# A two-block transformer on one core: paired attention heads in turns, split weight products in another order, later gates, routing without GpSimd

## The chip, the cores and the metric

The kernel runs on one core of a Trainium2 chip. The time is that of the device for one execution, in microseconds (us), as the median of the runs shown below. A core has a matrix engine (TensorE, PE in the profile), a vector engine (VectorE, DVE), a scalar engine (ScalarE, ACT), a general one (GpSimd, POOL), and a queue that issues the transfers (SyncE, SP). Each engine takes its instructions in the order of its own list and waits on semaphores for the others.

## The reference

The input is 256 tokens of 1024 columns. Everything is fp32.

```python
for l in range(2):
    x = x + 0.5 * swiglu(rmsnorm(x, ffn1_norm[l]), wg, wu, wd)      # d_ff 2816
    h = rmsnorm(x, mix_norm[l]) @ w_in[l]
    o = concat([mla(h_a), nsa(h_b), diff(h_c)])                      # 6, 6 and 4 heads
    x = x + o @ w_out[l]
    x = x + 0.5 * swiglu(rmsnorm(x, ffn2_norm[l]), wg, wu, wd)
h = concat([meta_tokens, rmsnorm(x, final_norm)])                    # 16 + 256 tokens
p = rmsnorm(h, norm_mix_2) @ w_in_2                                  # z, x, B, C, dt, b, c, h
y = concat([group_norm(ssd(x, B, C, dt) * silu(z)), group_norm(b * conv(c * h))])
h = h + y @ w_out_2
u = rmsnorm(h, norm_ffn_2)                                           # 4 groups x 4 experts, top 2 of one group
h = h + sum_e combine[:, e] * ((silu(u @ w_gate[e]) * (u @ w_up[e])) @ w_down[e])
out = rmsnorm(h, norm_final_2)[16:]
```

## The kernel before

**Split products.** A product of fp32 operands is made of three: each weight tile arrives as `st`, ScalarE rounds it to a high half `wh` (line 166), VectorE, or GpSimd for the tiles that the table `LOW` names, subtracts to get the low half `wl` (line 167). The activations have halves as well (`xhl`, `ohl`, `uhl`, `hh` and `hl`). `mm3` multiplies wh by the high half, wh by the low half, and wl by the high half, 256 columns each. `mm2` has both halves of the activations side by side: wh by 512 columns, wl by 256; the result then lies in two parts of a bank, and VectorE adds both.

**Order.** The code is written as tasks, and a scheduler orders the instructions of each engine; `behind(i)` holds what stands in it until the instruction i has been placed. TensorE does nearly all work: FFN1, the mixer (projection `win`, heads, `w_out`) and FFN2 for both layers, then the second block and the experts.

**The heads.** The softmax of a head gives a transposed P in a tile `PT`. The products of PT and the values of two heads go into one bank `opair`, one head in its partitions 0 to 63, the other in 64 to 127 (`pv_pair`). In the heads of NSA the products of the compressed branch (`cpt`) go into the same two halves. The fp32 products there are made in several passes, so one line of code is several matmul rows of the profile.

**From w_out to FFN2.** `w_out` makes eight tiles `wo` of 128x256, which VectorE adds to the residual stream `xT` (lines 966 and 967). From xT come the operand pieces `xhl` (lines 267 and 268) and the squares for the norm. Where FFN2 begins, its first four weight tiles are multiplied k by k into four `gu` banks, and two of these banks lie in the PSUM space of wo.

**The second block** follows the table `PART2`: step "z" makes the z columns, "u" the normed operand (xT times two factors gives `u`, its halves are `uhl`), "r" rewrites xT by the final norm of the first block, "d" the dt columns, "b", "x" the convolved ones (`proj`, then `cv`), "w" the last product. The z gate is tanh on ScalarE (`zth`) and a scalar_tensor_tensor on VectorE (line 1106).

**Routing.** `moe_tokens` runs for each half of the tokens: two copies, the sum of squares and its inverse root (`mss`, `mr`), eight transposes (`h2T`, copied to `hT`), eight products for the `logits`. `moe` splits the tokens into hh (ScalarE) and hl (GpSimd, line 1615), finds ranks and `slots`, gathers (`xgp`), and starts the experts' sum `moe` with identity products of the tokens. Those of the second half of the tokens are held behind the last logits product.

```python
            for k in KO:
                self.mm2(p, wh[:, k], wl[:, k], ohl[:, k], k == KO[0], k == KO[7])
            xv = self.xT[:, 2 * b + j]
            nc.vector.tensor_add(xv, p[:, 0:T], xv)
            nc.vector.tensor_add(xv, p[:, T:2 * T], xv)
```

## Time and profile before

| | before |
|---|---|
| median of 3 runs | 1568.68 us |
| lowest and highest run | 1567.85 and 1570.5 us |
| the profiled execution | 1569.35 us |
| its span, first to last instruction | 1567.5 us |
| mean granted TensorE clock (1 is 2.4 GHz) | 0.986 |

The profiled execution is one run of the same program. Its span is what the trace shows; the rest of its time, 1.85 us, lies around it. A granted clock of 0.50 in a stretch means that TensorE ran at 1.2 GHz there.

### The profile page before, as it was taken

How to read it: one execution, taken by the hardware profiler on the slowest of the kernel's cores; microseconds unless marked ns; L12 is line 12 of the kernel's file. 1: busy time of each engine (PE TensorE's matmuls, PEld its weight loads, DVE VectorE, ACT ScalarE, POOL GpSimd, SP SyncE). 2: the span in 40 equal slices, each digit the busy share in tenths (PEclk: the TensorE clock that was granted, in tenths of full speed). 3: DMA queues.
4: the chain of work that ended last, by engine and by line, in shares of the span. 5: the costliest groups of instructions: out<-in, count | busy, mean ns of one | idle time of the engine just before them, and what ended most of it. 6: DMA issues, size and time to landing. Idle time of an engine off the chain costs nothing.

```text
span 1567.5 us, 25184 instructions
## 1 busy us (share of the span) xinstructions
PE 1514.2 (97%) x9842; PEld 1256.1 (80%) x9842; DVE 1035.7 (66%) x2024; ACT 731.1 (47%) x1385; POOL 96.5 (6%) x144
## 2 busy tenths in 40 slices
PE   8999999999999999999999899999799999999996
PEld 7999998768999989999886799999799987344432
DVE  7777776857677886777585777778988875122112
ACT  5555465745445555545664554557554442011011
POOL 0000000600000000000033000000410101000000
PEclk9999999999999999999999999999999998999998
DMA  7756664125555565656530455566443588999992
GB/s 249 247 183 193 176 169 143 47 66 175 188 189 183 167 191 187 193 191 175 161 108 1 148 183 189 181 195 207 149 135 108 175 297 334 338 394 392 392 396 87
DMA packets 223558, 308.92 MB, mean 197 GB/s; under 512 B 20908, under 2 KB 167608, under 8 KB 223432
## 3 DMA queue, kind: packets, MB, share of 16 engines
q1 hardware_dynamic: 223128, 306.71, 58.7%
q8 instruction: 79, 1.29, 0.4%
q10 hardware_dynamic: 304, 0.53, 0.1%
q14 instruction: 47, 0.39, 0.1%
HBM read 306.16 MB, written 1.05 MB: 196 GB/s over the span
## 4 chain that ended last, share of the span: by engine, by line
PE 91%; DVE 6%; ACT 1%; issue 1%; DMA 0%; POOL 0%; ACTq 0%; DVEq 0%
PE gu L98 32%; PE acc L98 16%; PE proj L98 7%; PE win L98 6%; PE gate L98 4%; PE y L98 4%; PE up L98 4%; PE h L98 3%; PE S L98 3%; PE opair L98 2%; PE wo L98 2%; PE zp L98 1%; DVE wl L167 1%; PE moe L98 1%; PE ptp L684 1%; PE xgp L98 1%
## 5 line engine op out<-in xcount | busy, mean ns | idle before, releaser
L167 DVE TENSOR_TENSOR wl<-st,wh 128x1024 fp32r<-128x1024 f32 (+1 forms) x370 | 447.5, 1219 | 209.4 <-ACT wh L166 198.6
L166 ACT ACTIVATE wh<-st 128x1024 fp32r<-128x1024 f32 (+1 forms) x382 | 399.2, 1059 | 346.2 <-PE gu L98 136.4
L98 PE MATMUL gu<-xhl,wh 128*128 128x512 f32 (+1 forms) x1440 | 496.3, 394 | 14.1 <-DVE xT L967 11.0
L98 PE MATMUL gu<-xhl,wl 128*128 128x256 f32 x1408 | 390.5, 281 | 0.0
L98 PEld LDWEIGHTS gu<-xhl,wh 128*128 128x128 f32 x1440 | 269.6, 191 | 74.2 <-issue 12.4
L98 PEld LDWEIGHTS gu<-xhl,wl 128*128 128x128 f32 x1408 | 266.0, 190 | 0.1
L98 PE MATMUL acc<-hx,wh 128*128 128x256 f32 x1408 | 252.1, 281 | 0.0
L98 PEld LDWEIGHTS acc<-hx,wh 128*128 128x128 f32 x1408 | 216.4, 189 | 1.6
L98 PE MATMUL acc<-hx,wl 128*128 128x256 f32 x704 | 197.0, 281 | 0.0
L98 PE MATMUL proj<-uhl,wh 128*128 128x272 f32 (+2 forms) x592 | 129.0, 309 | 7.2 <-DVE cv L1208 5.1
L98 PEld LDWEIGHTS acc<-hx,wl 128*128 128x128 f32 x704 | 132.7, 189 | 0.0
L98 PE MATMUL win<-wh,xhl 128*128 128x256 f32 (+1 forms) x576 | 109.5, 286 | 0.2 <-DVE xT L403 0.2
L98 PEld LDWEIGHTS proj<-uhl,wh 128*128 128x128 f32 x592 | 97.5, 195 | 12.3 <-ACT zth L1105 4.4
L98 PE MATMUL proj<-uhl,wl 128*128 128x272 f32 (+2 forms) x328 | 96.2, 294 | 0.0
L98 PEld LDWEIGHTS win<-wh,xhl 128*128 128x128 f32 x576 | 90.9, 191 | 3.8 <-issue 3.1
L98 PE MATMUL win<-wl,xhl 128*128 128x256 f32 (+1 forms) x288 | 82.2, 285 | 0.0
L387 ACT ACTIVATE hx<-up 128x512 fp32r<-128x512 f32 x44 | 27.8, 631 | 87.8 <-DVE up L386 87.8
L98 PEld LDWEIGHTS proj<-uhl,wl 128*128 128x128 f32 x328 | 63.5, 194 | 0.3
L726 POOL TENSOR_SCALAR P<-P,mx 128x128 f32<-128x128 f32 (+2 forms) x88 | 53.2, 620 | 65.4 <-DVE mx L719 46.2
L1790 DVE SCALAR_TENSOR_TENSOR ys<-y,rc,ys 128x512 fp32r<-128x512 f32 x16 | 11.8, 749 | 68.5 <-ACT ys L1607 68.0
L716 ACT ACTIVATE P<-S,mx 128x256 f32<-128x256 f32 (+2 forms) x128 | 48.8, 396 | 17.5 <-DVE mx L712 4.4
L98 PEld LDWEIGHTS win<-wl,xhl 128*128 128x128 f32 x288 | 55.0, 191 | 0.6 <-issue 0.3
(523 smaller groups left out, 2158.3 us busy)
## 6 DMA issues: line engine op xcount, KB each, us to landing
st<-ffn_wg SPq DMA_DIRECT2D x44, 1024.0 KB, 5.8
st<-ffn_wu SPq DMA_DIRECT2D x44, 1024.0 KB, 5.4
st<-ffn_wd SPq DMA_DIRECT2D x44, 1024.0 KB, 4.9
st<-w_in SPq DMA_DIRECT2D x36, 1024.0 KB, 5.4
st<-w_out SPq DMA_DIRECT2D x16, 1024.0 KB
mf<-expert_w_gate SPq DMA_DIRECT2D x25, 512.0 KB, 9.5
mf<-expert_w_down SPq DMA_DIRECT2D x21, 512.0 KB, 10.7
mf<-expert_w_up SPq DMA_DIRECT2D x18, 512.0 KB, 11.3
```

Of the source, the lines that this page charges most:

```text
L98: return self.nc.tensor.matmul(out, lhsT, rhs, start=start, stop=stop, skip_group_check=True)
L166: hi = self.nc.scalar.activation(hl[0], src, AF.Copy)
L167: sub = (self.nc.gpsimd if lo[i] == "p" else self.nc.vector).tensor_sub(hl[1], src, hl[0].bitcast(F32))
L387: nc.scalar.activation(hh, up, AF.Copy)
L684: tr(p[:, i * 128:(i + 1) * 128], b, ident)
L716: nc.scalar.activation(P[:, d], s[:, c], AF.Exp, bias=m[:, 0, i:i + 1], accum_out=m[:, 1, i:i + 1])
L726: (nc.gpsimd if key + str(i) in "c0 c1 c2 d0 d1 m0 w0 w1".split() else nc.vector).tensor_scalar(P[:, d], P[:, d], r[:, i:i + 1], None, op0 ...
L1790: V.scalar_tensor_tensor(yl, py[half], rc[:, 1:2], yh.bitcast(F32), op0=OP.mult, op1=OP.subtract)
```

## The change

1. The products of a pair of heads stand together in TensorE's list: the products of the half 64 to 127 lead, and all others of the pair stand behind the first of them (`in_turns`). The compressed products are treated in the same way.
2. At the head of FFN2 (and of the second FFN1) the sixteen wh products of k 0 to 3 come first, then their sixteen wl products, then k 4 to 7 bank by bank.
3. `w_out` uses `mm3`, so that VectorE has one addition for each tile instead of two.
4. The tanh and the multiplication of the z gates become a step "q" behind x0, "r" moves to the end of its part, and their `behind(done)` goes.
5. `moe_tokens` does both halves: all hT copies on ScalarE, squares of the first half on ScalarE, hl on VectorE, all logits in one go, and all identity products held behind the last logits product.

```diff
@@ -31,9 +31,9 @@
 
 
 
-PART2 = ("z10 u z2 z3 d p4 b0 d r b1 d b2 b3 x0 x1 x2 s0 s0 x3 s0 c0 "
+PART2 = ("z10 u z2 z3 d p4 b0 d b1 d b2 b3 x0 q x1 x2 s0 s0 x3 s0 c0 "
          "h0 s1 s1 g0 s1 s2 s2 n0 c1 h1 s2 s3 g1 n1 s3 c2 h2 g2 s3 "
-         "| c3 h3 p5 g3 n2 y a w6 t0 t1 p7 t2 w0 n3 t3 % w1 p4 w5 w2 w4 p5 w3 w7")
+         "r | c3 h3 p5 g3 n2 y a w6 t0 t1 p7 t2 w0 n3 t3 % w1 p4 w5 w2 w4 p5 w3 w7")
 
 LOW = {k: "pp" for k in ["b3", "x0", "x1", "x2", "x3"]}
 LOW.update({k: "vp" for k in ["h3", "g2"]})
@@ -347,9 +347,16 @@
 
                 ws = [w for u in units for w in self.split(u, "n")]
                 ps = [self.bank(tag, "gu") for tag in "BBCC"]
-                for k, i in ([(k, i) for k in range(4) for i in range(4)]
-                             + [(k, i) for i in range(4) for k in range(4, KD)]):
-                    self.mm2(ps[i], ws[i][0][:, k], ws[i][1][:, k], xhl[:, k], k == 0, k == KD - 1)
+                high = lambda k, i: self.mm(ps[i], ws[i][0][:, k], xhl[:, k], k == 0, False)
+                low = lambda k, i: self.mm(ps[i][:, 0:T], ws[i][1][:, k], xh[:, k], False, k == KD - 1)
+                for part in (high, low):
+                    for k in range(4):
+                        for i in range(4):
+                            part(k, i)
+                for i in range(4):
+                    for k in range(4, KD):
+                        high(k, i)
+                        low(k, i)
                 return ps
             for i, u in enumerate(units):
                 for f, (wh, wl) in enumerate(self.split(u, "n", "vv")):
@@ -520,7 +527,7 @@
             return ap.tile([128, 2, n], F32, name=name, tag=tag or name, bufs=bufs)
 
         hA, hQ, hV, hC, hW = tok("hA", 352), tok("hQ", 768), tok("hV", 402), tok("hC", 512), tok("hW", 256)
-        oh, ol, ohl = self.pair("ohl")
+        oh, ol, _ = self.pair("ohl")
         B0, C0 = 352, 1522
         q0, kc0, vc0, ks0, vs0, kw0, vw0 = [B0 + c for c in (0, 384, 512, 640, 768, 896, 1024)]
         groups = [
@@ -697,11 +704,17 @@
 
         def pv_pair(o, key, first, last):
 
-            two = list(zip((o[0:64], o[64:128]), waiting.pop(key)))
-            for o_, (pt, v) in two:
-                self.mm(o_[:, 0:256], v[0], pt[:, 0:256], first, False)
-            for o_, (pt, v) in two:
-                self.mm(o_[:, 128:256], v[1], pt[:, 256:384], False, last)
+
+            two = list(zip((o[64:128], o[0:64]), waiting.pop(key)[::-1]))
+            in_turns([lambda o_=o_, pt=pt, v=v: self.mm(o_[:, 0:256], v[0], pt[:, 0:256], first, False) for o_, (pt, v) in two]
+                     + [lambda o_=o_, pt=pt, v=v: self.mm(o_[:, 128:256], v[1], pt[:, 256:384], False, last) for o_, (pt, v) in two])
+
+        def in_turns(products):
+
+            lead = products[0]()
+            with self.behind(lead.ins):
+                for product in products[1:]:
+                    product()
 
         def softmax(s, P, segs, gate=None, low=None):
 
@@ -854,8 +867,9 @@
             if h % 2:
                 o = self.bank("O", "opair")
                 pv_pair(o, "s", True, False)
-                for i, (c, v) in enumerate(waiting.pop("c")):
-                    self.mm(o[i * 64:(i + 1) * 64, 0:256], v, c[0:15], False, False)
+                c0, c1 = waiting.pop("c")
+                in_turns([lambda o_=o_, c=c: self.mm(o_, c[1], c[0][0:15], False, False)
+                          for o_, c in ((o[64:128, 0:256], c1), (o[0:64, 0:256], c0))])
             s = self.bank("S", "S")
             scores(s, qt, kw[:, g], kw[:, g, 0:128])
             P = ap.tile([128, 384], F32, name="P", tag="P", bufs=6)
@@ -961,10 +975,9 @@
             for j, (wh, wl) in enumerate(self.split(wo[b], "n")):
                 p = self.bank("WS"[j], "wo")
                 for k in KO:
-                    self.mm2(p, wh[:, k], wl[:, k], ohl[:, k], k == KO[0], k == KO[7])
+                    self.mm3(p[:, 0:T], wh[:, k], wl[:, k], oh[:, k], ol[:, k], k == KO[0], k == KO[7])
                 xv = self.xT[:, 2 * b + j]
                 nc.vector.tensor_add(xv, p[:, 0:T], xv)
-                nc.vector.tensor_add(xv, p[:, T:2 * T], xv)
             after(b)
 
 
@@ -1099,8 +1112,12 @@
         def z_gates(ids, ps):
             for b, p in zip(ids, ps):
                 for t in range(2):
+                    ACT(z[:, t, b * 256:(b + 1) * 256], p[:, t * 256:(t + 1) * 256], scale=R[:, t:t + 1])
+
+        def z_silu():
+            for b in range(4):
+                for t in range(2):
                     zv = z[:, t, b * 256:(b + 1) * 256]
-                    ACT(zv, p[:, t * 256:(t + 1) * 256], scale=R[:, t:t + 1])
                     th = ap.tile([128, 256], F32, name="zth", tag="zth", bufs=2)
                     nc.scalar.activation(th, zv, AF.Tanh, scale=0.5)
                     nc.vector.scalar_tensor_tensor(zv, th, 1.0, zv, op0=OP.add, op1=OP.mult)
@@ -1115,8 +1132,7 @@
                 u = ap.tile([128, T], F32, name="u", tag="q", bufs=4)
                 nc.vector.scalar_tensor_tensor(u, self.xT[:, k], self.gfm[:, k:k + 1], rb[:, 1], op0=OP.mult, op1=OP.mult)
                 ACT(uh[:, k, NM:], u)
-                low_u = nc.vector.tensor_sub(ul[:, k, NM:], u, uh[:, k, NM:].bitcast(F32))
-            return low_u.ins
+                nc.vector.tensor_sub(ul[:, k, NM:], u, uh[:, k, NM:].bitcast(F32))
 
         def residual_norm():
             for k in range(KD):
@@ -1409,16 +1425,15 @@
                 if k == "z":
                     zs = z_blocks([int(c) for c in name[1:]])
                     if len(zs[0]) == 1:
-                        with self.behind(done):
-                            z_gates(*zs)
+                        z_gates(*zs)
                 elif k == "u":
                     norms()
-                    done = u_operand()
-                    with self.behind(done):
-                        z_gates(*zs)
+                    u_operand()
+                    z_gates(*zs)
+                elif k == "q":
+                    z_silu()
                 elif k == "r":
-                    with self.behind(done):
-                        residual_norm()
+                    residual_norm()
                 elif k == "d":
                     next(parts)
                 elif k == "b":
@@ -1453,8 +1468,7 @@
             self.operands.close()
             self.xp = self.pool(self.ctx, "operands2", side="right")
             self.moe_start(acc)
-            for t in range(2):
-                self.moe_tokens(t)
+            self.moe_tokens()
             yield
 
         return run()
@@ -1579,24 +1593,37 @@
         self.r = self.ap.tile([128, 2], F32, name="mr", tag="mr")
         self.logits = self.bank("C", "logits")
 
-    def moe_tokens(self, t):
+    def moe_tokens(self):
 
         nc, V, h2, hT, acc = self.nc, self.nc.vector, self.h2, self.hT, self.acc
-        V.tensor_copy(h2[:, t, 0:512], acc[t][0])
-        V.tensor_copy(h2[:, t, 512:1024], acc[t][1])
-        self.moe_sumsq(t, 0, self.th_)
-        self.moe_sumsq(t, 1, self.ht_)
-        self.moe_inv(t)
-        for k in range(0, KD, 4):
-            p = self.bank("B", "h2T")
-            for i in range(4):
-                nc.tensor.transpose(p[:, i * 128:(i + 1) * 128], h2[:, t, (k + i) * 128:(k + i + 1) * 128], self.identr[:].bitcast(F32))
-            (V.tensor_copy if t and not k else nc.scalar.copy)(hT[:, k:k + 4, t * 128:(t + 1) * 128],
-                                                               p[:].rearrange("p (k t) -> p k t", k=4))
-        for k in range(KD):
-            last = self.mm(self.logits[:, t * 20:(t + 1) * 20], hT[:, k, t * 128:(t + 1) * 128], self.gw[:, k],
-                           t == 0 and k == 0, k == KD - 1)
+        half = lambda i: slice(i * 512, (i + 1) * 512)
+        for t in range(2):
+            for i in range(2):
+                V.tensor_copy(h2[:, t, half(i)], acc[t][i])
+            if t == 0:
+                for i, j in enumerate((self.th_, self.ht_)):
+                    nc.scalar.activation(j, h2[:, t, half(i)], AF.Square, accum_out=self.ss[:, 2 * i + t:2 * i + t + 1])
+            for k in range(0, KD, 4):
+                p = self.bank("B", "h2T")
+                for i in range(4):
+                    nc.tensor.transpose(p[:, i * 128:(i + 1) * 128], h2[:, t, (k + i) * 128:(k + i + 1) * 128], self.identr[:].bitcast(F32))
+                nc.scalar.copy(hT[:, k:k + 4, t * 128:(t + 1) * 128], p[:].rearrange("p (k t) -> p k t", k=4))
+            if t:
+                for i, j in enumerate((self.th_, self.ht_)):
+                    V.scalar_tensor_tensor(j, h2[:, t, half(i)], 1.0, h2[:, t, half(i)], op0=OP.mult, op1=OP.mult,
+                                           accum_out=self.ss[:, 2 * i + t:2 * i + t + 1])
+            self.moe_inv(t)
+        for t in range(2):
+            for k in range(KD):
+                last = self.mm(self.logits[:, t * 20:(t + 1) * 20], hT[:, k, t * 128:(t + 1) * 128], self.gw[:, k],
+                               t == 0 and k == 0, k == KD - 1)
         self.routed = last.ins
+        for t in range(2):
+            nc.scalar.activation(self.hh[:, t], h2[:, t], AF.Copy)
+        self.low_half(0)
+
+    def low_half(self, t):
+        self.nc.vector.tensor_sub(self.hl[:, t], self.h2[:, t], self.hh[:, t].bitcast(F32))
 
     def moe(self):
 
@@ -1609,10 +1636,6 @@
                                                         self.slots_, self.th_, self.ht_)
         sm = ap.tile([128, 346], F32, name="route", tag="route")
         p = self.logits
-
-        for t in range(2):
-            ACT(hh[:, t], h2[:, t])
-            nc.gpsimd.tensor_sub(hl[:, t], h2[:, t], hh[:, t].bitcast(F32))
         units = self.load_pair(0)
 
 
@@ -1648,6 +1671,7 @@
         Ab = ap.tile([128, 2, 16], BF, name="Ab", tag="Ab")
         V.scalar_tensor_tensor(Ab[:].rearrange("p t (g e) -> p t g e", g=4), pe, 2.0,
                                og[:, :, :, None].to_broadcast([128, 2, 4, 4]), op0=OP.is_lt, op1=OP.mult)
+        self.low_half(1)
         p = self.bank("C", "rank")
         self.mm(p[:, 0:16], self.below, Ab[:, 0], True, False)
         self.mm(p[:, 16:32], self.onesb, Ab[:, 0], False, False)
@@ -1717,7 +1741,7 @@
 
         acc = self.acc = [[self.bank("A", f"moe{t}{i}") for i in range(2)] for t in range(2)]
         for t in range(2):
-            with self.behind(*((self.routed,) if t else ())):
+            with self.behind(self.routed):
                 for half in range(2):
                     self.mm(acc[t][half], ident, h2[:, t, half * 512:(half + 1) * 512], True, False)
 
```

The first place is TensorE's list in the NSA heads of layer 0; opair rows are the products of a pair, ptp the transposes of P, S the scores. Before, with the lead product of this pair 25 rows further up:

```order
L98 MATMUL S<-maskb,identb 128x128
L98 MATMUL opair<-PT,hV 64x256
L98 MATMUL opair<-PT,hV 64x128 x2
L98 MATMUL opair<-cpt,vcmp 64x256
L684 MATMUL ptp<-ident,P 128x128 x3
L98 MATMUL opair<-cpt,vcmp 64x256
L98 MATMUL opair<-PT,hV 64x256
```

After:

```order
L98 MATMUL S<-maskb,identb 128x128
L98 MATMUL opair<-PT,hV 64x256 x2
L98 MATMUL opair<-PT,hV 64x128 x2
L691 MATMUL ptp<-ident,P 128x128 x3
L98 MATMUL opair<-cpt,vcmp 64x256 x2
L691 MATMUL ptp<-ident,P 128x128 x3
```

The lead product now stands with the other of its size (`x2`), the two 128-column products follow, and the two cpt products stand together. Of the nine PT pairs of a layer eight were separated before and none is now; all three cpt pairs were separated.

The second place is VectorE's list at the end of layer 0's w_out: xT rows are the additions, xhl the low halves of the operand of FFN2. Before:

```order
L966 TENSOR_TENSOR xT<-wo,xT 128x256
L167 TENSOR_TENSOR wl<-st,wh 128x1024
L966 TENSOR_TENSOR xT<-wo,xT 128x256
L967 TENSOR_TENSOR xT<-wo,xT 128x256
L167 TENSOR_TENSOR wl<-st,wh 128x1024
L967 TENSOR_TENSOR xT<-wo,xT 128x256
L167 TENSOR_TENSOR wl<-st,wh 128x1024
L967 TENSOR_TENSOR xT<-wo,xT 128x256
L167 TENSOR_TENSOR wl<-st,wh 128x1024
L966 TENSOR_TENSOR xT<-wo,xT 128x256
L268 SCALAR_TENSOR_TENSOR xhl<-xT,v_1109,xhl 128x256
L167 TENSOR_TENSOR wl<-st,wh 128x1024
```

After:

```order
L980 TENSOR_TENSOR xT<-wo,xT 128x256 x5
L167 TENSOR_TENSOR wl<-st,wh 128x1024 x3
L268 SCALAR_TENSOR_TENSOR xhl<-xT,v_1109,xhl 128x256
L980 TENSOR_TENSOR xT<-wo,xT 128x256
L167 TENSOR_TENSOR wl<-st,wh 128x1024
L268 SCALAR_TENSOR_TENSOR xhl<-xT,v_1109,xhl 128x256
L167 TENSOR_TENSOR wl<-st,wh 128x1024
L268 SCALAR_TENSOR_TENSOR xhl<-xT,v_1109,xhl 128x256 x2
L980 TENSOR_TENSOR xT<-wo,xT 128x256
L268 SCALAR_TENSOR_TENSOR xhl<-xT,v_1109,xhl 128x256
L167 TENSOR_TENSOR wl<-st,wh 128x1024
L268 SCALAR_TENSOR_TENSOR xhl<-xT,v_1109,xhl 128x256
```

The additions of a layer are eight instead of sixteen, and those that free the banks of gu's third and fourth tile, the sixth and the seventh, have three and five wl rows ahead of them; the last additions that freed these banks before stand further down, behind seven and eight.

The third place is VectorE's list at the head of the second block, from the copy of the row factors on. Before:

```order
L1080 COPY rb<-rbb 128x512
L1116 SCALAR_TENSOR_TENSOR u<-xT,gfm,rb 128x256 x4
L167 TENSOR_TENSOR wl<-st,wh 128x1024
L1118 TENSOR_TENSOR uhl<-u,uhl 128x256 x4
L1116 SCALAR_TENSOR_TENSOR u<-xT,gfm,rb 128x256 x3
L167 TENSOR_TENSOR wl<-st,wh 128x1024
L1116 SCALAR_TENSOR_TENSOR u<-xT,gfm,rb 128x256
L167 TENSOR_TENSOR wl<-st,wh 128x1024
L1118 TENSOR_TENSOR uhl<-u,uhl 128x256 x3
L167 TENSOR_TENSOR wl<-st,wh 128x1024
L1118 TENSOR_TENSOR uhl<-u,uhl 128x256
L1106 SCALAR_TENSOR_TENSOR z<-zth,z 128x256 x2
```

After:

```order
L1093 COPY rb<-rbb 128x512
L1133 SCALAR_TENSOR_TENSOR u<-xT,gfm,rb 128x256 x4
L1139 SCALAR_TENSOR_TENSOR xT<-xT,v_1109,rb 128x256 x2
L167 TENSOR_TENSOR wl<-st,wh 128x1024
L1139 SCALAR_TENSOR_TENSOR xT<-xT,v_1109,rb 128x256
L1123 SCALAR_TENSOR_TENSOR z<-zth,z 128x256
L1139 SCALAR_TENSOR_TENSOR xT<-xT,v_1109,rb 128x256
L1123 SCALAR_TENSOR_TENSOR z<-zth,z 128x256
L1135 TENSOR_TENSOR uhl<-u,uhl 128x256 x4
```

Four rows of the rewriting of xT and two z gates now stand ahead of the first low half of uhl; before, all of them stood behind the last.

## Rows read from the trace of the kernel before

**Rows 1.** First part of the page: busy time, share of the span, instructions

```profile
PE 1514.2 (97%) x9842; PEld 1256.1 (80%) x9842; DVE 1035.7 (66%) x2024; ACT 731.1 (47%) x1385; POOL 96.5 (6%) x144
```

**Rows 2.** Waits of PE: releaser, us in total, times, longest us

```profile
PE gu L98 <- DVE xT L967: 11.0, 4, 3.5
PE proj L98 <- DVE cv L1208: 5.1, 2, 4.2
...
PE logits L98 <- DVE hT L1594: 2.6, 1, 2.6
```

**Rows 3.** Timeline of PE, end of layer 0's w_out: start, us, engine, line, tile

```profile
347.66 0.40 PE L98 MATMUL wo<-ohl,wh 128*128 128x512 f32 x1
...
348.01 0.39 PE L98 MATMUL gu<-xhl,wh 128*128 128x512 f32 x1
...
352.40 0.76 PE L98 MATMUL gu<-xhl,wh 128*128 128x512 f32 x1 [3.53 <-DVE xT L967]
...
355.19 0.77 PE L98 MATMUL gu<-xhl,wh 128*128 128x512 f32 x1 [1.81 <-DVE xT L967]
```

**Rows 4.** Windows behind w_out: us, busy of each engine (x), PEclk, DMA share

```profile
352.40:359.20 6.80, 4.99 (x15) 3.93 (x16) 5.79 (x12) 2.45 (x5) 0.00 (x0) 0.51 0.81 253
...
882.80:888.20 5.40, 5.40 (x17) 4.63 (x18) 2.95 (x7) 1.37 (x3) 0.00 (x0) 0.50 0.62 192
```

**Rows 5.** DVE groups of tile wo, and of the low halves (from the page)

```profile
L966 DVE TENSOR_TENSOR xT<-wo,xT x16: 413/416/425, 338.3 to 880.1; 128x256 f32<-128x256 f32 x16
...
L167 DVE TENSOR_TENSOR wl<-st,wh 128x1024 fp32r<-128x1024 f32 (+1 forms) x370 | 447.5, 1219 | 209.4 <-ACT wh L166 198.6
```

**Rows 6.** Timeline of PE: one pair of heads at 258, one at 294

```profile
258.32 0.87 PE L98 MATMUL opair<-PT,vm 128*64 128x256 f32 x8
259.12 0.39 PE L98 MATMUL win<-wl,xhl 128*128 128x256 f32 x1
...
294.10 0.65 PE L98 MATMUL opair<-PT,hV 128*64 128x256 f32 x2
294.67 0.73 PE L98 MATMUL S<-ks,qT 128*128 128x272 f32 x2
...
298.09 0.86 PE L98 MATMUL opair<-PT,hV 128*64 128x256 f32 x6
298.89 0.64 PE L98 MATMUL opair<-cpt,vcmp 15*64 15x256 f32 x2
```

**Rows 7.** Window in the attention heads of layer 0

```profile
285.00:300.00 15.00, 15.00 (x113) 11.83 (x112) 13.15 (x60) 11.57 (x55) 9.01 (x15) 1.00 0.01 2
```

**Rows 8.** Timeline of PE in an FFN's down products

```profile
50.30 0.40 PE L98 MATMUL acc<-hx,wh 128*128 128x256 f32 x2
...
51.01 0.40 PE L98 MATMUL acc<-hx,wh 128*128 128x256 f32 x2
```

**Rows 9.** DVE groups of 1089 to 1112, then timelines of POOL, DVE and PE

```profile
L1123 DVE SCALAR_TENSOR_TENSOR xT<-xT,v,rb 128x256 f32<-128x256 f32 x8 | 3.3, 482 | 0.0
...
1105.63 7.64 POOL L167 TENSOR_TENSOR wl<-st,wh 128x1024 fp32r<-128x1024 f32 x3 [260.21 <-ACT wh L166]
...
1106.04 0.50 DVE L1208 SCALAR_TENSOR_TENSOR cv<-proj,v,cv 128x271 f32<-128x271 f32 x1
...
1107.30 3.76 DVE L1106 SCALAR_TENSOR_TENSOR z<-zth,z 128x256 f32<-128x256 f32 x2 [0.76 <-ACT zth L1105]
...
1112.14 0.80 PE L98 MATMUL proj<-uhl,wh 128*128 128x272 f32 x2 [4.23 <-DVE cv L1208]
```

**Rows 10.** Timeline of the routing: PE, DVE, PE, DVE

```profile
1313.88 1.88 PE L98 MATMUL moe<-h,identr 128*128 128x512 f32 x4
...
1318.03 2.23 DVE L1567 SCALAR_TENSOR_TENSOR mr<-mss 128x1 f32<-128x1 f32 x1
...
1323.71 3.76 PE L98 MATMUL moe<-h,identr 128*128 128x512 f32 x4
...
1329.06 0.17 DVE L1708 TENSOR_TENSOR route<-route 128x8 f32<-128x8 f32 x1
```

## The prediction

> **What bounds the kernel now.** The first part of the page says that TensorE is busy for 1514 us of the 1567.5 us span, 97% [rows 1]; VectorE has 66%, and no other engine stands for the whole. A change can therefore win in two ways: TensorE has less to do, or it waits less. I next read the list of what TensorE waited for. Three rows of it belong to places that the diff touches: four waits of gu for the additions of w_out, 11.0 us, two of proj for the convolution's VectorE work, 5.1 us, and one of the logits for a copy, 2.6 us [rows 2]. Then I read the timeline at each place to see what stands ahead of the late instruction, and the granted clock behind it.
>
> At the end of layer 0's w_out TensorE starts gu at 348.01, has two of the four banks, waits 3.53 us for the third and 1.81 us for the fourth [rows 3]. What it waits for is not weights: the releaser is line 967, the second addition of a wo tile, whose bank gu wants. Behind these waits the clock is at 0.50, the lower level, for 6.8 us in layer 0 and 5.4 us in layer 1 [rows 4]. A wait here is paid twice.
>
> **Part by part.** *w_out with one addition.* VectorE loses 16 additions of 0.416 us, eight in each layer; in the same stretch it has eight low halves of 1.22 us each [rows 5]. More than the sum, the order counts: in the list of after, the additions that free gu's third and fourth bank have three and five low halves ahead of them, not seven and eight. From the first addition at 338.3 the fourth bank costs 7 x 0.416 + 5 x 1.22 + 5 x 0.47 (xhl, whose duration I take near the addition's) = 11.4 us if nothing overlapped, so it is free at 349.7 at the latest; the start of one instruction overlaps the end of the last by 0.08 us, which makes it 348.3. gu wants it at 348.01 + 3 x 0.24 = 348.7. So the 11.0 us of waits go: **-11.0 us**. Next late would be xhl for k 4 to 7 and the low halves of the weights; the new order asks for the low ones only behind sixteen high products, some 3.7 us after gu's start (16 x 0.23, two thirds of mm2's 0.35). In the old order the fourth bank's low half, the sixth in VectorE's list, would be asked for at once and be late by one more instruction, 1.2 us.
>
> With the waits gone I expect the clock to stay up, as it did in the stretch ahead. TensorE did 4.98 us (the window's PE column) and 5.40 us of work at half clock [rows 4]; half of each is lost: **-5.2 us**. If a wait of some tenths remains this may still hold; if a microsecond or two remains, I would count none of it.
>
> The price is on TensorE: mm3 makes three matmuls of 256 columns for each of 128 k-steps instead of one of 512 and one of 256. One mm2 takes 348.01 - 347.66 = 0.35 us [rows 3]. Six products of 256 columns, each with its own weights, take 51.01 - 50.30 = 0.71 us, 0.118 us each [rows 8], so mm3 takes 0.355 us. The difference is at most 0.01 us: 128 x 0.01 = **+1.3 us**.
>
> *The heads in turns.* A pair whose products stand together takes 259.12 - 258.32 = 0.80 us. Where another head's work stands between, the lead alone takes 294.67 - 294.10 = 0.57 us, and the rest, six rows instead of eight, still 298.89 - 298.09 = 0.80 us [rows 6]. So the lead beside its partner costs nothing: the two halves of the array run at the same time. Eight of nine PT pairs in a layer are put together, and three cpt pairs, whose single products I price like a lead: 11 x 0.57 = 6.3 us a layer, 12.5 us in all, on an engine that is full there (15.00 of 15 us [rows 7]). That is the upper bound. The lower one is nothing: VectorE is busy for 13.15 of the same 15 us, ScalarE for 11.57 and GpSimd for 9.01, so that the softmax may set the pace as soon as TensorE is faster, and the leads are the work that filled TensorE's time while it did. VectorE has 12% to spare, and 6.3 us is 12% of the 53 us from 285 to 338; both say that the engines then end about together, so I take half: **-6.3 us**.
>
> *Gates and rewriting.* Before, the conv stalls since two z multiplications take 3.76 us where GpSimd works on low halves (1105.63 to 1113.27): 4.23 us of wait [rows 9]. After, the gates stand earlier and this goes, with the other wait of this kind: -5.1 us. But four xT rows and two z rows now stand ahead of the first uhl, and as many again among the rest, although the code moves "r" far back: the scheduler takes them early since nothing holds them any more. An xT row is 3.3 / 8 = 0.41 us, and VectorE has no idle time around them [rows 9]; 12 x 0.41 = 4.9 us of delay reach the last uhl, which proj reads in that order. Below, it is nothing if proj comes later than that; VectorE is full there, so I take 4.1 us of new wait: **-1.0 us**.
>
> *Routing.* GpSimd's hl stretches a VectorE instruction on a single column to 2.23 us [rows 10], and the copy to hT behind it is what the logits wait for. Without GpSimd this goes: -2.6 us. Against it: slots stand behind the whole chain of the expert weights now, about 13 instructions of 0.17 us [rows 10], +2.2 us. All identity products lie in that time, under the route chain, where at half clock they take 3.76 us for the same work as 1.88 us; I count half of the difference as won, -1.0 us. Together **-1.4 us**; bounds -4.5 us (no wait, no half clock) and +2.2 us (VectorE's own two low halves, 1.22 us each, take the place of the wait).
>
> **The sum**: -11.0 - 5.2 + 1.3 - 6.3 - 1.0 - 1.4 = -23.6 us on the profiled execution's 1569.35 us: 1545.7. That execution was 0.67 us above the median of the runs shown, so the forecast is 1545 us.
>
> **The rivals.**
> 1. *The heads' saving doesn't reach the end.* For it speaks VectorE's 88% in that stretch; against it, that TensorE had no wait there. Then 1545 + 6.3 = 1551 us. Or all of it does: 1539 us.
> 2. *The wait at gu moves on to xhl or wl.* VectorE's work from 338.3 on is 8 x 0.416 + 8 x 1.22 + 8 x 0.47 = 16.8 us, 15 us with 24 overlaps of 0.08 us, so the last xhl comes about at 353 to 354, and gu wants it some 6 us after 348. If 2 us of wait remain in each layer, the clock falls as before: 4 + 5.2 us, 1554 us.
> 3. *The gates meet GpSimd.* Four of the z rows stand behind the last uhl. If they reach 1105.6, each takes 1.9 us instead of 0.4 us beside GpSimd, 6 us, and the wait at proj is back on top of the new one: 1545 + 6 = 1551 us. The order puts them ahead of the first cv, which in the trace came at 1106.04 and took 0.50 us, with one source in PSUM [rows 9]. The Trainium skill (GPSIMD Engine Reference, section Specifications) says that GpSimd shares its SBUF interfaces with VectorE, to the cost of VectorE instructions with two SBUF inputs; by that rule the rewriting of xT and the gates are both at risk wherever they meet a low half of GpSimd, and this rival is the outcome. The trace agrees for z, 1.9 us; xT never met one.
> 4. *Slower: the leads make TensorE wait.* All 24 runs of opair products now start when the later head's PT is there, and what stands behind in TensorE's list waits too. If rival 1 holds and each run waits w, the time is 1551 + 24 w; it is slower than before by 0.2% from w = 0.86 us on, and at 1 us it gives 1575 us. Against it: the rest of each pair stood at that same place and waited for the same PT without a gap that the window shows.
> 5. *The change does nothing that counts*: the additions were moved, but gu's waits stay in another form, and the heads win nothing: 1568 us.
>
> **How the numbers follow.** The sum with its own spread (1541 to 1549): 0.46. Rival 1: 0.18 for 1551, and 0.12 for 1539. Rival 2: 0.13. Rival 3: 0.05. Rival 4: 0.03. Rival 5: 0.03. The range takes in rivals 1 to 3 and a little on either side, 1536 to 1556; it leaves out the two last and some of the ends. About 0.2%, 3 us, is what a measurement of this kernel can tell from no change: faster 0.94, same 0.03, slower 0.03.
>
> **What would show it.** In the profile of after: no row gu <- xT above 1 us, and a granted clock of 1 behind both w_outs; opair in 24 runs of 0.8 us or less, cpt pairs at about 0.6 us, and the time from the first head to the end of w_out some 3 us shorter in a layer; three wo products in 0.355 us; a wait of proj for uhl of 1 to 4 us between the dt columns and the first cv, and none for cv; the logits without a wait of 2 us, and one of about 2 us for the slots. I would be wrong above all if the clock stays low behind w_out though the waits are gone, or if TensorE shows new gaps between the scores of the heads.

## The result: 1531 us, 38 us less than before and below the range

| | before | changed |
|---|---|---|
| median | 1569.01 us (4 runs) | 1531.46 us (4 runs) |
| lowest and highest run | 1567.85 and 1570.5 us | 1530.11 and 1532.0 us |
| span of the profiled execution | 1567.5 us | 1529.8 us |
| mean granted clock | 0.986 | 0.994 |

The ratio is 0.9759, with a 95% interval of 0.9742 to 0.9776. The forecast was 1545 us, with a range from 1536 to 1556 us. The sign and most places were right, but the gain was 38 us where 23.6 us were summed up.

The first part of the page of the changed kernel answers to [rows 1]:

```profile
PE 1492.0 (98%) x9970; PEld 1253.6 (82%) x9970; DVE 1025.1 (67%) x2013; ACT 729.7 (48%) x1382; POOL 91.4 (6%) x142
```

TensorE has 128 instructions more (w_out makes three products where it made two) and is busy for 22 us less. The waits of TensorE, which answer to [rows 2], with the releaser, us in total, times and the longest:

```profile
PE gu L98 <- ACT wh L166: 2.2, 1, 2.2
...
PE proj L98 <- DVE dv L1184: 1.6, 1, 1.6
PE btok L1244 <- DVE BC L1227: 1.4, 1, 1.4
PE proj L98 <- DVE uhl L1135: 1.3, 1, 1.3
...
PE xgp L98 <- DVE slots L1693: 0.8, 1, 0.8
PE proj L98 <- DVE cv L1224: 0.8, 1, 0.8
...
PE proj L98 <- ACT z L1050: 0.7, 1, 0.7
```

The four waits of gu for xT are gone, the one of the logits too, and those of proj for cv fell from 5.1 to 0.8 us. Waits for uhl, 1.3 us, and for z, 0.7 us, are new, and those for dv and BC grew from 1.2 and 0.2 us to 1.6 and 1.4 us. Where w_out ends, the timeline and the windows of the changed kernel answer to [rows 3, 4]; the window's columns end with granted clock, DMA share and GB/s:

```profile
341.96 0.28 PE L98 MATMUL wo<-ohl,wl 128*128 128x256 f32 x1
342.08 1.78 PE L98 MATMUL gu<-xhl,wh 128*128 128x512 f32 x7
```

```profile
342.00:349.00 7.00, 7.00 (x42) 6.17 (x42) 6.90 (x12) 3.96 (x7) 0.00 (x0) 1.00 0.86 291
...
854.90:862.00 7.10, 7.10 (x43) 6.22 (x42) 7.00 (x12) 4.12 (x8) 0.00 (x0) 1.00 0.83 284
```

The high products follow w_out without a gap (the timeline's window ends after seven of the sixteen), TensorE is busy for 7.00 of 7 us, and the clock stays at 1.00. In the heads the timeline answers to [rows 6]:

```profile
297.92 0.87 PE L98 MATMUL opair<-PT,hV 128*64 128x256 f32 x8
298.73 0.55 PE L691 MATMUL ptp<-ident,P 128*128 128x128 f32 x3
299.20 0.65 PE L98 MATMUL opair<-cpt,vcmp 15*64 15x256 f32 x4
299.78 0.44 PE L691 MATMUL ptp<-ident,P 128*128 128x128 f32 x2
```

A PT pair takes 298.73 - 297.92 = 0.81 us, a cpt pair 299.78 - 299.20 = 0.58 us, and all 24 runs look alike.

To find where the time came from I cut each trace at the first instruction of a stage. The table gives the length of each stage in us, from the starts in the timelines, for the two kernels and the experiments that undo one part (e1 to e5) or do one part alone on the kernel before (e6):

| stage, from | before | changed | e1 pairs | e2 adds | e3 gu | e4 routing | e5 gates | e6 turns alone |
|---|---|---|---|---|---|---|---|---|
| start to first win | 200.4 | 201.6 | 200.0 | 201.2 | 200.5 | 201.2 | 200.5 | 200.0 |
| mixer, layer 0 | 147.6 | 140.5 | 147.3 | 140.5 | 140.5 | 140.5 | 140.5 | 142.8 |
| FFN2 and next FFN1 | 380.5 | 372.7 | 372.7 | 381.7 | 373.4 | 372.7 | 372.7 | 381.1 |
| mixer, layer 1 | 147.1 | 140.0 | 146.9 | 139.9 | 140.0 | 140.0 | 140.0 | 140.0 |
| FFN2, layer 1 | 194.3 | 185.9 | 185.9 | 195.3 | 186.1 | 185.9 | 185.9 | 193.4 |
| first zp to acp | 65.5 | 62.8 | 63.2 | 63.4 | 63.1 | 62.8 | 66.3 | 64.9 |
| acp to h2T | 177.6 | 177.9 | 176.6 | 176.4 | 176.5 | 177.8 | 177.6 | 177.5 |
| routing, h2T to gate | 21.0 | 18.0 | 18.0 | 17.9 | 18.0 | 20.9 | 18.0 | 20.0 |
| gate to the end | 233.5 | 230.5 | 230.5 | 230.6 | 230.5 | 232.7 | 230.6 | 233.9 |

By stages the 37.7 us of the span are: mixers -14.2, FFN stages -16.1, gates (first zp to acp) -2.8, routing -3.0, experts -3.0, and +1.4 in stretches that the change doesn't touch. In the mixers, the FFN stages, the routing and the experts, a stage that e1 to e5 leave alone comes out within 0.2 us of the changed kernel's, so that each of these rows reads like an experiment of its own. Elsewhere traces of the same code differ by more: the start by 1.6 us, the stretch from acp to h2T by 1.5 us, the stage from zp to acp by 0.6 us.

### The profile page after: what moved, and what is told of

It is laid out like the page before. It is cut to its first block, busy times and chain, and to the rows that moved or that the text cites. A ratio compares the mean times of both kernels' runs of the same rounds, so it can differ in the third digit from the quotient of the medians.

```text
span 1529.8 us, 25415 instructions
## 1 busy us (share of the span) xinstructions
PE 1492.0 (98%) x9970; PEld 1253.6 (82%) x9970; DVE 1025.1 (67%) x2013; ACT 729.7 (48%) x1382; POOL 91.4 (6%) x142
## 4 chain that ended last, share of the span: by engine, by line
PE 92%; DVE 5%; ACT 1%; issue 1%; DMA 0%; POOL 0%; ACTq 0%; DVEq 0%
PE gu L98 32%; PE acc L98 16%; PE proj L98 6%; PE win L98 6%; PE gate L98 4%; PE y L98 4%; PE up L98 4%; PE h L98 3%; PE wo L98 3%; PE S L98 3%; PE moe L98 1%; PE opair L98 1%; PE ptp L691 1%; PE zp L98 1%; PE xgp L98 1%; DVE wl L167 1%
## 5 line engine op out<-in xcount | busy, mean ns | idle before, releaser
L98 PE MATMUL gu<-xhl,wh 128*128 128x512 f32 (+1 forms) x1440 | 487.8, 392 | 3.1 <-ACT wh L166 2.2
L98 PE MATMUL gu<-xhl,wl 128*128 128x256 f32 x1408 | 381.6, 280 | 0.0
L98 PEld LDWEIGHTS gu<-xhl,wl 128*128 128x128 f32 x1408 | 260.8, 189 | 0.3
L1814 DVE SCALAR_TENSOR_TENSOR ys<-y,rc,ys 128x512 fp32r<-128x512 f32 x16 | 11.7, 749 | 67.2 <-ACT ys L1634 66.8
```

The source lines that it names most:

```text
L98: return self.nc.tensor.matmul(out, lhsT, rhs, start=start, stop=stop, skip_group_check=True)
L1814: V.scalar_tensor_tensor(yl, py[half], rc[:, 1:2], yh.bitcast(F32), op0=OP.mult, op1=OP.subtract)
```

## The experiments

**e1: the pairs apart again.** The changed kernel with the old pair products.

```diff
-            two = list(zip((o[64:128], o[0:64]), waiting.pop(key)[::-1]))
-            in_turns([lambda o_=o_, pt=pt, v=v: self.mm(o_[:, 0:256], v[0], pt[:, 0:256], first, False) for o_, (pt, v) in two]
-                     + [lambda o_=o_, pt=pt, v=v: self.mm(o_[:, 128:256], v[1], pt[:, 256:384], False, last) for o_, (pt, v) in two])
+            two = list(zip((o[0:64], o[64:128]), waiting.pop(key)))
+            for o_, (pt, v) in two:
+                self.mm(o_[:, 0:256], v[0], pt[:, 0:256], first, False)
+            for o_, (pt, v) in two:
+                self.mm(o_[:, 128:256], v[1], pt[:, 256:384], False, last)
...
```

The compressed products, not shown here, go back in the same way.

> The changed kernel, with the products of a pair of heads as before (no turns). If every separated lead costs TensorE its 0.57 us in full, 11 in a layer, the time from the first win product to gu grows by 6 to 8 us in each layer and the whole by 12 to 16 us, to about 1545 us, a ratio to before near 0.985. The rival, that the mixer became shorter since VectorE has fewer additions and half of the heads' saving is lost to the softmax, gives back at most 6 us: about 1537 us. opair is then in 34 runs again.

Measured: 1543.18 us, ratio to before 0.984 (0.9823 to 0.9856). The mixers are back at 147.3 and 146.9 us, 13.7 us together, and no other stage is more than 0.4 us longer. The median is 11.7 us above the changed kernel's, 2 us less than the mixers; in that trace the start is 1.6 us and the stretch from acp 1.3 us shorter. The heads' saving arrives whole.

**e6: the turns alone**, on the kernel before (the reverse of e1's diff).

> The kernel before, with the pairs in turns and nothing else. If the heads' saving reaches the end whole, 12.5 us of opair and some 2.5 us of the transposes beside them: 1569 - 15 = 1554 us. If softmax takes half of it, 1562 us. gu's waits for the additions stay, 11 us in four.

Measured: 1555.68 us, 0.9917 (0.9902 to 0.9932), 13 us less than before. The mixers take 142.8 and 140.0 us; in layer 0 the clock was at 0.50 from 273.5 to 280.3, which no other trace has there but e9's, from 274.0 to 277.4. The heads need no other part of the change for their gain.

**e12: less work in the heads.** The changed kernel without the products of cpt with the values, so that the compressed branch is missing from the attention's output.

```diff
-                c0, c1 = waiting.pop("c")
-                in_turns([lambda o_=o_, c=c: self.mm(o_, c[1], c[0][0:15], False, False)
-                          for o_, c in ((o[64:128, 0:256], c1), (o[0:64, 0:256], c0))])
+                waiting.pop("c")
```

> The changed kernel, which leaves out the products of the compressed branch with their values (its share is missing from the attention's output): six runs of opair of 0.58 us in both layers. If TensorE still sets the pace of the heads, the time falls by 3.5 us or a little more, to 1528 us, and no wait appears. If the softmax had become the limit, TensorE waits at the scores or the transposes for as much, and the time stays at 1531 us.

Measured: 1527.17 us, 0.9731 (0.9716 to 0.9745), 4.3 us less than the changed kernel. The mixers take 138.6 and 138.1 us, 1.9 us less each, for three runs of 0.58 us. TensorE still sets the pace of the heads; there is one new wait:

```profile
PE opair L98 <- DVE PT L876: 0.6, 2, 0.3
```

Softmax was not the limit that I had taken it for.

**e7: a pair head by head.** The four products of a pair together, but in the order of the heads.

```diff
-            in_turns([lambda o_=o_, pt=pt, v=v: self.mm(o_[:, 0:256], v[0], pt[:, 0:256], first, False) for o_, (pt, v) in two]
...
+            in_turns([lambda o_=o_, p=p, v=v, c=c, i=i: self.mm(o_[:, c], v[i], p, first and i == 0, last and i == 1)
+                      for o_, (pt, v) in two
+                      for i, c, p in ((0, slice(0, 256), pt[:, 0:256]), (1, slice(128, 256), pt[:, 256:384]))])
```

> The changed kernel, with a pair's products together but head by head (both of the lead's, then both of the other's). If the two halves of the array run at the same time only where products of both halves alternate, a pair takes about 1.25 us instead of 0.80, 18 pairs, and the time grows by 8 us to 1539 us. If what costs is only the passage from other work to 64-column products and back, a pair still takes 0.80 us and the time stays.

Measured: 1530.7 us, 0.9758 (0.9743 to 0.9773), the same as the changed kernel. The timeline of TensorE in e7:

```profile
296.59 0.88 PE L98 MATMUL opair<-PT,hV 128*64 128x256 f32 x8
297.40 0.55 PE L691 MATMUL ptp<-ident,P 128*128 128x128 f32 x3
```

The pair still takes 0.81 us. So the products needn't alternate; they need only have nothing else between them. The halves still run at the same time: the first two rows of the pair start 14 ns apart (7 ns in the changed kernel), while the two passes of a lone product start 0.27 us apart in the kernel before. The rows don't name the head, so that these two belong to different heads is read from the times.

**e2: w_out with two additions.** The changed kernel with mm2 in w_out.

```diff
...
-                    self.mm3(p[:, 0:T], wh[:, k], wl[:, k], oh[:, k], ol[:, k], k == KO[0], k == KO[7])
+                    self.mm2(p, wh[:, k], wl[:, k], ohl[:, k], k == KO[0], k == KO[7])
                 nc.vector.tensor_add(xv, p[:, 0:T], xv)
+                nc.vector.tensor_add(xv, p[:, T:2 * T], xv)
```

> The changed kernel, with w_out by mm2 and two additions for each tile. If gu's waits went because the additions that free its banks stand further up in VectorE's list, they come back with the low clock behind them: 11 + 5 us less 1.5 us of matmuls, about 1546 us. If the new order of gu's products is what took them away, the time stays within 2 us of 1531.

Measured: 1548.65 us, 0.987 (0.9853 to 0.9886), 17 us above the changed kernel. Waits of TensorE and the window behind layer 0's wait in e2:

```profile
PE gu L98 <- DVE xT L981: 12.0, 4, 3.8
```

```profile
347.50:354.20 6.70, 5.24 (x12) 4.12 (x13) 4.46 (x10) 1.54 (x3) 0.00 (x0) 0.50 0.52 173
```

All four waits are back, and the clock is at 0.50 behind them. The two FFN stages grew by 18.4 us: 12.0 of waits, and most of the rest is clock (5.24 us of work at 0.50 in layer 0 and 6.66 us in layer 1, from 866.2 to 876.5; half of it is 6.0 us). In e2 both the number of additions and their place in VectorE's list go back, so the run doesn't say which of the two counts. The mixers are as long as in the changed kernel (140.5 and 139.9 us), but that doesn't make mm3 free. The rows of wo in layer 1, before and in the changed kernel, are:

```profile
728.51:875.59 147.08, 24.23 (x128) 1.00 0.33 99
714.78:854.76 139.98, 25.51 (x192) 1.00 0.36 107
```

The columns are the window, its length, TensorE's busy time on wo, the clock, DMA share and GB/s. From the start of each row to the start of the next, w_out takes 0.7 us less in e2 than in the changed kernel in each layer, and transposes and scores, which stand in another order there, take about as much more.

**e3: gu's old order.** The changed kernel with the first products k by k.

```diff
...
-                for part in (high, low):
-                    for k in range(4):
-                        for i in range(4):
-                            part(k, i)
...
+                for k, i in ([(k, i) for k in range(4) for i in range(4)]
+                             + [(k, i) for i in range(4) for k in range(4, KD)]):
+                    self.mm2(ps[i], ws[i][0][:, k], ws[i][1][:, k], xhl[:, k], k == 0, k == KD - 1)
```

> The changed kernel, with gu's first products k by k as before. If the additions alone free gu, at most the wait for late low halves appears: 0 to 2.5 us in a layer, 1531 to 1536 us. If the high products first are what fills TensorE's time until the low halves are there, waits of 3 us or more and a low clock come back behind each w_out: 1540 us or more.

Measured: 1531.51 us, 0.9766 (0.975 to 0.9783): no difference. The FFN stages are 0.7 and 0.2 us longer, and one wait is new:

```profile
PE gu L98 <- DVE wl L167: 0.6, 2, 0.3
```

Once the additions are early, the low halves are late for the old order by 0.3 us twice, and by nothing for the new one.

**e5: gates and rewriting as before.**

```diff
-PART2 = ("z10 u z2 z3 d p4 b0 d b1 d b2 b3 x0 q x1 x2 s0 s0 x3 s0 c0 "
+PART2 = ("z10 u z2 z3 d p4 b0 d r b1 d b2 b3 x0 x1 x2 s0 s0 x3 s0 c0 "
...
-                    u_operand()
-                    z_gates(*zs)
+                    done = u_operand()
+                    with self.behind(done):
+                        z_gates(*zs)
...
```

The tanh and the multiplication go back into `z_gates`, and r stands behind(done) again.

> The changed kernel, with the z gates and the rewriting of the residual as before, held behind the last uhl. By the traces this part is worth 2.7 us, most of it the clock behind the 4.2 us wait: about 1534 us, with that wait and z rows of over 1.2 us beside GpSimd again. If the stage now starts at another moment against GpSimd, the z rows may miss it and the time stays at 1531 us.

Measured: 1533.36 us, 0.977 (0.9755 to 0.9785). The stage takes 66.3 us instead of 62.8; the medians alone, 1.9 us apart, don't separate the two kernels. TensorE's wait and a VectorE row of its timeline:

```profile
PE proj L98 <- DVE cv L1221: 5.1, 2, 4.2
```

```profile
1077.08 3.77 DVE L1119 SCALAR_TENSOR_TENSOR z<-zth,z 128x256 f32<-128x256 f32 x2 [0.76 <-ACT zth L1118]
```

Two z rows beside GpSimd, whose low halves run from 1075.41 to 1083.07, take 3.77 us once more, and the clock is at 0.50 from 1080.7 to 1087.5.

**e9: only the rewriting held.** The changed kernel, with step r behind the last uhl.

```diff
...
-                    residual_norm()
+                    with self.behind(done):
+                        residual_norm()
```

> The changed kernel, with the rewriting of xT (step r) held behind the last uhl again and the gates as they are. If the xT rows ahead of uhl are what proj waits for, its waits for uhl and z, 2.0 us, shrink by a microsecond or more and the time falls to 1530 us. If the z rows alone or ScalarE's halves set them, nothing changes.

Measured: 1528.32 us, 0.9744 (0.9729 to 0.976). The stage takes 61.2 us, 1.6 us less. The waits of proj for uhl, z and dv are gone from TensorE's list, and another stands in it:

```profile
PE proj L98 <- ACT bmeta L1050: 1.7, 1, 1.7
```

e11 below, with the same edit, takes 61.4 us in this stage, and e10, without it, 63.1 us. The median is 3 us lower than the changed kernel's, but the five runs go from 1526.2 to 1532.5 us, and the interval overlaps; in the trace the routing stage, whose code the edit doesn't touch, is shorter by 3.3 us (below). The edit is worth its 1.6 us by the stage; a faster version by the median isn't shown.

**e4: the old routing** (moe_tokens, GpSimd's hl and the `behind` of the identity products as in the kernel before).

```diff
...
-        for t in range(2):
-            nc.scalar.activation(self.hh[:, t], h2[:, t], AF.Copy)
-        self.low_half(0)
...
+        for t in range(2):
+            ACT(hh[:, t], h2[:, t])
+            nc.gpsimd.tensor_sub(hl[:, t], h2[:, t], hh[:, t].bitcast(F32))
...
-            with self.behind(self.routed):
+            with self.behind(*((self.routed,) if t else ())):
```

> The changed kernel, with routing as before: GpSimd's low halves, the tokens in two parts, half of the identity products ahead of the logits. By the traces routing is worth 3.0 us and the end of the experts another 1.9 us, where the order of the experts' y and stp products differs. If that order follows from the routing's, the time is 1536 us and the y products are split again; if not, 1534.5 us. The wait of the logits for hT, 2.6 us, returns in both.

Measured: 1536.04 us, 0.979 (0.9774 to 0.9806), 4.6 us above the changed kernel: 2.9 in the routing and 2.2 among the experts. TensorE's timeline near the end of the experts in e4, then in the changed kernel:

```profile
1490.96 0.33 PE L1746 MATMUL stp<-identr,slots 128*128 128x128 f32 x1
1491.23 1.93 PE L98 MATMUL y<-ms,acts 128*64 128x512 f32 x4
1493.09 0.33 PE L1746 MATMUL stp<-identr,slots 128*128 128x128 f32 x1
```

```profile
1485.75 2.80 PE L98 MATMUL y<-ms,acts 128*64 128x512 f32 x12
1488.48 0.44 PE L1756 MATMUL stp<-identr,slots 128*128 128x128 f32 x2
```

The y products use half of the array's columns (128*64 in the rows), like opair. With a transpose between them four y rows take 1.86 us, 0.47 us each; together, twelve take 2.73 us, 0.23 us each. The scheduler's order there, nearly 200 us later, comes from the routing code.

**e8, e10, e11: the identity products elsewhere.** In the changed kernel they stand ahead of rank:

```profile
1287.92 6.48 PE L98 MATMUL moe<-h,identr 128*128 128x512 f32 x8
...
1290.88 0.17 DVE L1672 SCALAR_TENSOR_TENSOR Ab<-route 128x32 bf16<-128x32 f32 x1
...
1294.24 0.17 PE L98 MATMUL rank<-Ab,below 128*128 128x16 bf16 x1
```

Ab, rank's operand, is there at 1291.05, and rank starts 3.2 us later, behind identity products that run mostly at half clock. e8 holds them behind rank, e10 holds those of the second half of the tokens behind the gather, and e11 is e10 with e9's edit.

In e8, where `ranked` is the last rank product:

```diff
-            with self.behind(self.routed):
+            with self.behind(ranked.ins):
```

In e10 and e11, where `gathered` is the last xgp product:

```diff
-            with self.behind(self.routed):
+            with self.behind(self.gathered.ins if t else self.routed):
```

> The changed kernel, with the identity products held behind the last rank product instead of the last logits product. In the trace of after they take 6.5 us, mostly at half clock, and rank waits for them for 3.2 us after its operand is ready. If they set the routing's length, slots come 1.5 to 3 us earlier and the time falls by as much, to 1529 us; if the products only move into the gather's way, nothing changes.

> The changed kernel, with the identity products of the first half of the tokens where they are (between logits and rank) and those of the second half behind the last xgp product. The first half fills the time until Ab is ready, and nothing stands ahead of xgp: rank about 3 us earlier, xgp 2 to 3 us earlier, 1.7 us of products later at full clock. The time falls by 1 to 2 us to about 1530 us; if the clock decides the stage, it stays.

> Both edits, of the rewriting held behind uhl and of the identity products split: the sum of their gains, 1528 to 1530 us, if the two stages are independent.

Measured: 1533.17 us, 0.977 (0.9757 to 0.9784); 1531.92 us, 0.9764 (0.975 to 0.9777); 1530.58 us, 0.9754 (0.9741 to 0.9768). None is faster. In e8 rank comes at 1290.02, and the gather then waits for the same products:

```profile
1290.02 0.17 PE L98 MATMUL rank<-Ab,below 128*128 128x16 bf16 x1 [3.00 <-DVE Ab L1672]
...
1290.15 6.52 PE L98 MATMUL moe<-h,identr 128*128 128x512 f32 x8
1296.11 0.68 PE L98 MATMUL xgp<-slots,hh 128*128 128x256 f32 x1
```

In e10 rank came early as well, and as in e8 and e11 the clock was at 0.50 for over 10 us of the stage, not for 6.9 us as in the changed kernel (1286.7 to 1293.6). The stage takes 20.2, 19.8 and 19.8 us in e8, e10 and e11. Windows of e10 and of e9, whose routing code is that of the changed kernel:

```profile
1284.00:1294.30 10.30, 9.44 (x37) 7.13 (x37) 7.13 (x49) 0.42 (x2) 0.00 (x0) 0.50 1.03 403
```

```profile
1280.50:1295.10 14.60, 13.44 (x94) 10.85 (x92) 13.86 (x64) 4.36 (x8) 0.00 (x0) 1.00 1.04 400
```

In e9's trace the clock didn't fall there, and the whole stage takes 14.7 us instead of 18.0. Two things are in this. e7 has the lists of the changed kernel on TensorE, VectorE and ScalarE in this stage, and its clock stayed at 1.00 as well: 16.5 us, so that the clock is worth 1.5 us. The rest is VectorE's list, in which the scheduler moved the slots in e9. The slots of e7, then of e9:

```profile
1292.26 0.76 DVE L1694 TENSOR_TENSOR slots<-slot,route 128x256 fp32r<-128x256 f32 x2
```

```profile
1290.59 0.76 DVE L1695 TENSOR_TENSOR slots<-slot,route 128x256 fp32r<-128x256 f32 x2
```

In both, rank starts at 1290.0 to 1290.1; in e7 the rows behind rank then wait for the chain of the expert weights, in e9 they stand ahead of most of it. Whether the longer half clock of e8, e10 and e11 comes from their order or from chance, these runs don't separate.

## Why the prediction was wrong, step by step

*The heads: the step that failed first.* "The softmax may set the pace as soon as TensorE is faster [...] so I take half: -6.3 us." I read VectorE's 88% as nearly full and halved the only price that the rows gave. The rows were exact: 11 separated products of 0.57 us in a layer, and from the start of each row to the start of the next opair takes 12.5 us less in both layers. The mixers gave 14.2 us, and e1 (13.7 us) and e6 (11.9 us, with half-clock time in one) say that the turns alone give it. Beyond opair, the transposes ptp and ptc take 1.5 us less in each layer, which I hadn't counted. Part of that is their place: directly ahead of or behind an opair row, a transpose's start is 0.17 to 0.20 us from the next start instead of 0.11, and fewer stand there now. w_out takes back 0.8 us in each layer. e12 shows that TensorE could be relieved of still more. With the upper bound the sum would have been 1538.8 us, which is rival 1's other end, to which I gave 0.12. That is still inside the range; it took the experts, the gates and the routing as well to fall below it.

*w_out.* Right, mechanism and size: -11.0 - 5.2 = -16.2 us forecast, -16.1 us in the two FFN stages. The additions are the cause (e2); gu's new order, which I made responsible for a wait of 1.2 us for a low half, saves 0.9 us in the two stages (e3). mm3's +1.3 us was right too: w_out's rows take 1.5 us more in both layers together, which the shorter mixers hide.

*Gates: the clock was put at nothing.* -2.8 us measured, -1.0 forecast. The two stages as windows, before and after:

```profile
1069.86:1135.41 65.55, 57.16 (x439) 55.40 (x438) 60.26 (x120) 41.56 (x81) 17.41 (x8) 0.95 0.59 189
```

```profile
1040.71:1103.50 62.79, 54.82 (x437) 53.05 (x436) 57.30 (x120) 41.90 (x81) 16.95 (x8) 1.00 0.62 198
```

The waits came out near the sum: 4.3 us of cv are gone, 2.0 us for uhl and z and 1.6 us more for BC and dv are new, so TensorE's time without work fell only from 8.4 to 8.0 us. The other 2.3 us are busy time, 57.16 against 54.82: before, the clock fell to 0.50 at 1110.0, within the wait of 4.23 us, and stayed there until 1116.9, with 4.76 us of work in that stretch; after, it stayed at 1.00. I had priced such a stretch behind w_out and none here. In other traces of the new order (e1, e3, e7, e10) 3.4 us at half clock are left and the stage takes 63.1 or 63.2 us. Rival 3 didn't occur: the last z row ended at 1077.3, GpSimd's low halves began at 1079.05. In e5 the gates stand where they stood, and z takes 1.9 us beside GpSimd again instead of 0.4. That agrees with the rule that rival 3 names from the Trainium skill (GPSIMD Engine Reference, section Specifications). In e9 a z row that ran in the first 0.4 us of a low half took 0.42 us, so that not every row there is slowed. For xT nothing shows it, since in no run a row of its rewriting stood beside GpSimd. Rival 2 didn't occur either: no wait for xhl or wl is in the list.

*Routing.* -3.0 us measured, -1.4 forecast. The slots, before and after:

```profile
1327.89 0.75 DVE L1669 TENSOR_TENSOR slots<-slot,route 128x256 fp32r<-128x256 f32 x2
```

```profile
1294.78 0.76 DVE L1693 TENSOR_TENSOR slots<-slot,route 128x256 fp32r<-128x256 f32 x2
```

From h2T to the identity products behind the last logits (1323.71 and 1287.92) it takes 4.1 us less: the wait of 2.6 us went, and four identity products no longer stand there. From these to the slots it takes 2.7 us more, 6.9 against 4.2, where I had +2.2; I called the identity products hidden "under the route chain", but at half clock they are longer than the chain, and rank stands behind them. With the clock up the chain is the longer one, 1.8 us (e7 against e9). From the slots to gate it takes 1.5 us less, since the gather came while the clock was up again, where I had -1.0.

*Experts: a term put at nothing.* -3.0 us, for which the sum had no term and gave no reason. 2.2 us follow from the routing code (e4) by the order of y and stp. The rest, 0.8 us, lies behind the last product, in the output's transfers, and no run separates it.

Of the 14 us between forecast and result 9 are the mixers, 3 the experts, 2 routing, 2 the gates, and 1.4 go the other way in untouched stretches.

## What to carry to other kernels

Products that use half of the array's columns belong next to each other, in either order that was tried, with nothing for the whole array between them: a lone compressed product took 0.57 us here, a pair of them 0.58 us. Where an engine has no wait and another is busy for 88%, don't halve a saving on the full one; ask what slack each item of the chain has, or take the bound that the rows give. When a wait of the matrix engine goes, look for a half-clock stretch behind it, at every place and not only at the largest: behind waits of 3.5 and 4.2 us it was there in the kernel before, among those of 1.6 us and less in the second block it was there in some traces and not in others. Where a product waits for a bank, look first at the additions that free it: making them fewer and earlier gave 17 us, reordering the products that wait at most 0.9 us.

## What the runs showed that was not expected

That two 64-column products run at the same time even when one head's whole series stands first in the list (e7, 0.81 us). The Trainium skill (TensorEngine Tiling (Array Packing), section Key Properties) says that tiles of the array operate independently, and that a change of the tiling mode drains the engine. The first agrees with the rows, 0.81 us for the eight rows of both heads; the second would explain why a lone product costs 0.57 us and why a ptp behind opair was slow, but no run here measured a drain by itself.

That the same lists get the full clock in one trace and half in another: the routing stage is 18.0 us long in most traces, with 6.9 us at a granted clock of 0.50, and 16.5 us in e7, with 1.00 throughout. In e9, again with 1.00 throughout, it is 14.7 us long by VectorE's other order.
